# Four modulation vectors of layer 0: from TensorE pieces to row products on VectorE

## The chip, the core and the metric

One Trainium2 chip, one core. The metric is the device time of one execution in microseconds (us), median of several runs. Engines are written PE (TensorE), ACT (ScalarE), DVE (VectorE), POOL (GpSimd) and SP (SyncE); each works through its own list of instructions in a fixed order. In a matmul row, "psg<-wr,cv" reads: into the PSUM tile psg, moving operand wr, stationary operand cv.

## The reference, cut to what matters

A first block (retention and a linear recurrence) gives x. Then two layers of a transformer work on x and on a context xc of 256 tokens each, width 1024. Each layer draws six vectors per sequence out of a condition vector; they scale, shift and gate the activations:

```python
for l in range(DEPTH_2):
    mod = (jax.nn.silu(c) @ w_mod[l] + b_mod[l])[:, None, :]      # 1024 x 6144
    mod_c = jax.nn.silu(c_ctx) @ w_mod[l] + b_mod[l]
    sh1, sc1, ga1, sh2, sc2, ga2 = jnp.split(mod, 6, axis=-1)
    csh1, csc1, cga1, csh2, csc2, cga2 = jnp.split(mod_c, 6, axis=-1)
    h = modulate(rms_norm_2(x, g_pre_mix[l]), sh1, sc1)           # and hc
    ...                                                           # mLSTM, GQA and NA branches, merged into o
    x = x + ga1 * rms_norm_2(o, g_post_mix[l])
    f = conv_ffn(modulate(rms_norm_2(x, g_pre_ffn[l]), sh2, sc2), w_up[l], conv_w[l], conv_b[l], w_down[l])
    x = x + ga2 * rms_norm_2(f, g_post_ffn[l])
```

The change is about ga1, sh2, sc2 and ga2 (numbers m = 2 to 5) of layer 0, for both condition vectors. The first, ga1, is needed only behind the mixers, the last only behind the feed-forward part.

## The kernel before, in words

Everything is fp32. A weight matrix is read in tiles of 128x1024 (512 KB) into `wr` (four buffers) by a DMA on SP's queue; ACT makes a rounded high part `wh` (L106), DVE the rest `wl` (L107), and PE forms three products for each pair of operands (`mm3`, L123 to L125). "The weights' split" below is this L106 and L107. Activations have the same two parts, `hh` and `hl`.

A layer's mixers run one behind the other: `gqa`, `mlstm`, `na`. Beside them runs a list of fillers (`Work`, with a `load` and a generator of short pieces): 24 gate matmuls (`gates`, weights `w_zg`, about 5 us of PE each, called zs in the code), the projections of the branches, and the modulation pieces. `fill(us)` steps fillers until their nominal microseconds are used up; `attend` calls it once for each of its 27 steps with `fills[1]`, and `gqa` once ahead of it with `fills[0]` (the table `FILLS`, L26). Instructions are written in program order, and the scheduler of the framework puts each engine's list in an order by that and by when it reckons the operands to be there; so PE's list around a wait is filled ahead of the run, and a late operand is then a wait.

**A modulation piece** (`modulation`, L363 to L394): for vector m and row block kt, a DMA on SP brings 128x1024 raw weights into `wr`, and four fp32 matmuls (L382) with the two condition vectors as a stationary 128x32 tile `cv` add to a PSUM bank. Behind the eighth piece ACT copies the bank out (L387) and `mod_end` (L409) turns it with two transposes (L419), adds `b_mod` (L423) into `modT`, and forms the gain (m = 1, 4) or the gate row (m = 2, 5; L433 to L438, with a transpose and a small DMA on POOL). Of layer 0, m = 0 and 1 are done in the first block; the 32 pieces of m = 2 to 5 are mixed into the gate matmuls, two to a gate, and run within `gqa`. `y` (the output of each mixer) has its two parts in the tiles yh and yl, six buffers each.

**The stages in time** (of the profile below): up to 240 us the first block; 240 to 281 us the queries and keys of `gqa` of layer 0 (q1, k1, k0, q0 in the code: 1 is the context, 0 is x; L839 to L904 and L808 to L883), in which DVE normalizes, rotates and splits them (`hs`) for PE to transpose (L881 keys, L902 queries); 281 to 431 us its attention with fillers; 431 to about 590 us `mlstm`, of which 431 to 508 are projections and 508 on its four heads; then `na`.

Of the kernel before, what the change touches and what calls it, by code (L numbers as in the profile page):

```python
# [25 lines left out]
FILLS = [(8.0, 3.6, 5.0), (4.0, 1.8, 2.5)]  # L26
# [4 lines left out]
STOCK_Y, STOCK_FIRST = 6, 2  # L31
NPARAM = 0
# [40 lines left out]
class Kern:  # L73
    def __init__(self, tc, A, es):
        self.tc, self.nc, self.A, self.es = tc, tc.nc, A, es
        self.n = 0
        self.cp = es.enter_context(tc.tile_pool(name="const", bufs=1))
        self.hp = es.enter_context(tc.tile_pool(name="h", bufs=1))
# [103 lines left out]
    def gemm_wide(self, src, x, seqs, order=None, at=None, parts=None):  # L182
# [7 lines left out]
        for i, k0 in enumerate(order):  # L190
# [27 lines left out]
    def step(self):  # L218
# [11 lines left out]
        try:  # L230
            self.credit -= next(self.cur[1])
# [131 lines left out]
    def modulation(self, l, pool=None):  # L363
# [3 lines left out]
        def load(m, kt):  # L367
            raw = self.mods[m * KT + kt].tile
# [3 lines left out]
            for i, t in enumerate(raw):  # L372
                self.nc.sync.dma_start(out=t, in_=self.A[f"w_mod{l}"][m * KT + kt][:, i * n : (i + 1) * n])
# [17 lines left out]
        self.mods = [Work(0.45, lambda w, m=m, kt=kt: piece(w, m, kt), lambda m=m, kt=kt: load(m, kt), ahead=l == 0 and m < 2) for m in range(6) for kt in range(KT)]  # L391
        self.fillers += self.mods

    def stock(self, works, pool, n, y=False):  # L394
# [3 lines left out]
        for w in some:  # L398
            if y:
                w.tile = [self.tl(pool, [P, 512], t, 6) for t in ("yh", "yl")]  # L400
            else:
                w.tile = [self.tl(pool, [P, 1024], "stock", n)]
        return some

    def fetch(self, works):
# [4 lines left out]
        return works  # L410

    def mod_end(self, l, m, row):
# [9 lines left out]
        for r in range(2):  # L422
            nc.vector.tensor_tensor(dst[:, :, :, r], src[:, :, :, r], bm[:, m * 8 : (m + 1) * 8].rearrange("p (j b) -> p j b", b=2), ALU.add)  # L423
        i = m // 3
        kind = ("mix", "ffn")[i]
        v = mt[:, 8 * m : 8 * m + 8]
        if m % 3 == 1:
            for r in range(2):
                nc.vector.scalar_tensor_tensor(self.sc[l][:, i, r], v[:, :, r], 1.0, self.param(f"g_pre_{kind}_2{l}"), ALU.add, ALU.mult)
        if m % 3 == 2:  # L430
            gg = self.tl(self.cp, [P, 2, 8], "mgate", 2)
            for r in range(2):
                nc.vector.tensor_tensor(gg[:, r], v[:, :, r], self.param(f"g_post_{kind}_2{l}"), ALU.mult)  # L433
            pt = self.bank("t", 2)
            nc.tensor.transpose(pt[:16, :P], gg.rearrange("p r k -> p (r k)"), self.idn)
            out = self.fs()[:16, :P]
            nc.vector.tensor_copy(out, pt[:16, :P])
            nc.gpsimd.dma_start(out=self.gd[l][2 * i : 2 * i + 2].rearrange("a (k p) -> (a k) p", p=P), in_=out)  # L438
# [5 lines left out]
    def first_block(self):  # L444
        nc, A, tc = self.nc, self.A, self.tc
        with ExitStack() as es:
# [45 lines left out]
            rest = self.fillers[2 * KT :]  # L492
            del self.fillers[2 * KT :]
# [59 lines left out]
            self.fillers += rest  # L553
# [224 lines left out]
    def new_y(self, nq):  # L778
        return [(self.tl(self.ap, [P, nq], "yh", 6, F32R), self.tl(self.ap, [P, nq], "yl", 6, F32R)) for _ in range(4)]

    def gqa(self, l, qs, fills):
        nc, A = self.nc, self.A
        y = self.new_y(len(qs) * T)
        with ExitStack() as es:
# [163 lines left out]
            self.attend(gp, [pair(s, pr) for s in qs for pr in range(4)], fills[1])  # L948
        return y
# [104 lines left out]
    def mlstm(self, l, qs, fills):  # L1054
        nc, A = self.nc, self.A
        y = self.new_y(len(qs) * T)
        nq = len(qs) * T
        with ExitStack() as es:
            mp = es.enter_context(self.tc.tile_pool(name=f"ml{l}", bufs=1))
            mlmask = self.load(mp, [P, 2, P], "mlmask", A["ml_mask"])  # L1060
# [49 lines left out]
            def prepare(h):  # L1110
# [17 lines left out]
                nc.scalar.activation(k, ps, AF.Copy, scale=P**-0.5)  # L1128
                return ub, dg, q, k
# [33 lines left out]
            self.require(self.br[0])  # L1163
            for s in qs:
                ss = self.tl(mp, [P, 8], "mss", 2)
                for t in range(2):
                    for h in range(4):
                        junk = self.tl(mp, [P, P], "mjunk", 1)
# [6 lines left out]
                for hp in range(2):  # L1175
# [380 lines left out]
```

## Time and profile before

| | |
|---|---|
| median of 3 runs | 1768.2 us (1767.57 to 1769.2) |
| the profiled execution, its own time | 1768.12 us |
| its span, first to last instruction | 1766.3 us |
| PE busy | 1730.1 us, 98% |
| DVE / ACT / POOL busy | 1118.3 (63%) / 877.4 (50%) / 130.0 us (7%) |
| granted TensorE clock, mean | 0.996 |
| share of PE in the chain that ended last | 86% |

A busy PE here counts each matmul from its start to its modelled end; matmuls overlap, so what one costs is read from the distance between starts. Busy shares are averages over stages; the sections below go by stage.

### The profile page before, as it was taken

The numbers are of one execution on the slowest core, as the hardware profiler recorded it, in microseconds if no ns is written. First come the engines' busy times: TensorE is split into PE (matmuls) and PEld (weight loads), VectorE is DVE, ScalarE is ACT, GpSimd is POOL, SyncE is SP. The second block draws the span as 40 slices with busy tenths as digits, with TensorE's granted clock in tenths as the row PEclk, the third lists the DMA queues.
The fourth block names the chain that finished last, engine by engine and source line by source line (L and its number), as shares of the span: only waits on it lengthen the run. The fifth ranks groups of instructions, "written<-read, shape, count | busy, mean of one in ns | idle before, by whom it ended". The sixth has DMA issues, their size and how long they took to land.

```text
span 1766.3 us, 27570 instructions
## 1 busy us (share of the span) xinstructions
PE 1730.1 (98%) x10512; PEld 1465.8 (83%) x10512; DVE 1118.3 (63%) x2159; ACT 877.4 (50%) x1597; POOL 130.0 (7%) x126
## 2 busy tenths in 40 slices
PE   7999999999999999999999999999999999989998
PEld 6889887777888887787778888888889888879987
DVE  7978676444435687558556663369744578578864
ACT  6665554344435455335434442346654456456652
POOL 2210000000100010000101110000010000002210
PEclk9999999999999999999999999999999999999999
DMA  8864544666334332553454334454446545876573
GB/s 300 292 202 146 168 157 154 213 197 224 120 115 137 114 106 87 171 198 138 166 171 130 100 102 137 132 188 146 136 140 201 160 149 159 294 243 191 180 226 106
DMA packets 111381, 295.66 MB, mean 167 GB/s; under 512 B 28144, under 2 KB 37936, under 8 KB 110992
## 3 DMA queue, kind: packets, MB, share of 16 engines
q1 hardware_dynamic: 110544, 292.96, 51.3%
q8 instruction: 83, 1.36, 0.3%
q0 software_dynamic: 272, 0.36, 0.1%
q10 hardware_dynamic: 432, 0.57, 0.1%
q14 instruction: 50, 0.41, 0.1%
HBM read 278.05 MB, written 19.46 MB: 168 GB/s over the span
## 4 chain that ended last, share of the span: by engine, by line
PE 86%; DVE 7%; DMA 3%; ACT 2%; issue 1%; SPq 1%; POOL 0%; DVEq 0%; ACTq 0%; POOLq 0%
PE psg L123 25%; PE psg L125 24%; PE psg L124 24%; DVE wl L107 2%; PE psg L764 2%; PE psg L382 2%; PE pst L750 2%; PE pst L1155 1%; PE pss L938 1%; PE pss L1027 1%; PE pss L1143 1%; DMA fs<-sigd 1%; DMA wr<-in_w_in_dram 1%; ACT wh L106 1%; DMA wr<-in_w_up_dram 1%
## 5 line engine op out<-in xcount | busy, mean ns | idle before, releaser
L107 DVE TENSOR_TENSOR wl<-wr,wh 128x1024 fp32r<-128x1024 f32 x359 | 443.9, 1239 | 319.4 <-ACT wh L106 306.4
L106 ACT CAST wh<-wr 128x1024 fp32r<-128x1024 f32 x360 | 375.8, 1045 | 414.2 <-PE psg L124 164.0
L123 PE MATMUL psg<-hh,wh 128*128 128x256 f32 (+1 forms) x1712 | 570.6, 334 | 1.6 <-ACT hh L322 1.0
L125 PE MATMUL psg<-hh,wl 128*128 128x256 f32 (+1 forms) x1712 | 562.7, 329 | 2.0 <-DVE wl L107 1.6
L124 PE MATMUL psg<-hl,wh 128*128 128x256 f32 (+1 forms) x1712 | 564.5, 330 | 0.0
L123 PEld LDWEIGHTS psg<-hh,wh 128*128 128x128 f32 x1712 | 325.7, 191 | 48.0 <-issue 11.4
L125 PEld LDWEIGHTS psg<-hh,wl 128*128 128x128 f32 x1712 | 325.5, 190 | 33.3 <-DVE wl L107 2.5
L124 PEld LDWEIGHTS psg<-hl,wh 128*128 128x128 f32 x1712 | 325.9, 190 | 28.3 <-DVE rstd L277 0.8
L123 PE MATMUL psg<-wh,hh 128*128 128x512 f32 (+1 forms) x320 | 118.7, 371 | 1.5 <-ACT fs L331 1.5
L124 PE MATMUL psg<-wl,hh 128*128 128x512 f32 (+1 forms) x320 | 118.5, 370 | 0.0
L125 PE MATMUL psg<-wh,hl 128*128 128x512 f32 (+1 forms) x320 | 118.4, 370 | 0.0
L1401 POOL TENSOR_TENSOR u<-u 128x512 f32<-128x512 f32 (+1 forms) x44 | 61.4, 1395 | 671.1 <-DVE u L1356 671.1
L125 PE MATMUL psg<-wh,midl 128*128 128x512 f32 (+1 forms) x276 | 101.6, 368 | 0.0
L123 PE MATMUL psg<-wh,midh 128*128 128x512 f32 (+1 forms) x276 | 101.5, 368 | 0.0
L124 PE MATMUL psg<-wl,midh 128*128 128x512 f32 (+1 forms) x276 | 101.5, 368 | 0.0
L1352 ACT ACTIVATE u<-psg,prm 128x256 f32<-128x256 f32 (+1 forms) x92 | 59.7, 649 | 27.9 <-PE psg L125 27.9
L123 PEld LDWEIGHTS psg<-wh,hh 128*128 128x128 f32 x320 | 60.4, 189 | 11.5 <-ACT fs L331 1.7
L731 ACT ACTIVATE p<-pss,sm 128x512 f32<-128x512 f32 x64 | 43.9, 687 | 49.9 <-DVE sm L730 49.7
L125 PEld LDWEIGHTS psg<-wh,hl 128*128 128x128 f32 x320 | 60.5, 189 | 9.7
L124 PEld LDWEIGHTS psg<-wl,hh 128*128 128x128 f32 x320 | 60.3, 189 | 9.6
L123 PE MATMUL psg<-yh,wh 128*128 128x512 f32 (+1 forms) x192 | 65.4, 341 | 0.0
L125 PE MATMUL psg<-yh,wl 128*128 128x512 f32 (+1 forms) x192 | 64.9, 338 | 0.0
(315 smaller groups left out, 2507.4 us busy)
## 6 DMA issues: line engine op xcount, KB each, us to landing
wr<-in_w_up_dram SPq DMA_DIRECT2D x88, 512.0 KB, 3.7
wr<-in_w_mod_dram SPq DMA_DIRECT2D x55, 512.0 KB, 4.1
wr<-in_w_zg_dram SPq DMA_DIRECT2D x48, 512.0 KB, 4.1
wr<-in_w_in_dram SPq DMA_DIRECT2D x40, 512.0 KB, 4.7
wr<-in_w_dw_dram SPq DMA_DIRECT2D x40, 512.0 KB, 3.5
wr<-in_w_br_dram SPq DMA_DIRECT2D x24, 512.0 KB, 3.5
stock<-in_w_mod_dram SPq DMA_DIRECT2D x19, 512.0 KB, 6.5
v<-in_w_mod_dram SPq DMA_DIRECT2D x16, 512.0 KB, 4.3
```

Source lines behind the costliest of these rows:

```text
L106: nc.scalar.copy(hi, raw)
L107: self.last_lo = (eng or nc.vector).tensor_tensor(lo, raw, hi.bitcast(F32), ALU.subtract).ins
L123: mm(ps, a[0], b[0], start=first, stop=False)
L124: mm(ps, a[0], b[1], start=False, stop=False)
L125: mm(ps, a[1], b[0], start=False, stop=last)
L382: nc.tensor.matmul(ps[32 * j : 32 * j + 32, 0:T], self.cv[:, kt], raw[j], start=kt == 0, stop=kt == KT - 1)
L731: nc.scalar.activation(t, s, AF.Exp, bias=m, accum_out=z)
L750: nc.tensor.transpose(pt[:, k * P : (k + 1) * P], t[:, k * P : (k + 1) * P], self.idn)
L764: nc.tensor.matmul(po[64 * j : 64 * j + 64, :T], p[2](j, k), pTs[id(p), j][:, k], start=k == 0, stop=k == nk - 1)
L938: nc.tensor.matmul(ps, qT[s, pr][:, j, qt * P : (qt + 1) * P], kT[kv][:, c, s * T : 512], start=c == 0, stop=c == 1)
L1352: nc.scalar.activation(u, ps, AF.Identity, scale=cw[:, 1, n : n + 1], bias=cb[:, n : n + 1])
L1401: nc.gpsimd.tensor_tensor(a, a, b, ALU.mult)
```

## The change

The pieces of m = 2 to 5 of layer 0 leave TensorE. Their weights are laid out transposed on the host (`w_mt0`: a row of 1024 inputs for each of the outputs, 128 outputs to a tile, 32 tiles of 512 KB). For each tile and each of the two condition vectors DVE runs one `scalar_tensor_tensor` (tile x 0.5 x row, with its sum over 1024 elements into a column of `modT`): 64 products. The row is silu(c) twice over, broadcast to 128 partitions, made by `mod_rows` within `gqa`: two DMAs on SP, four tanh on ACT, four DVE operations. The tiles come in through two buffers (`mw`) by DMAs on POOL's queue; a load waits for the two products that read the tile before it in its buffer. `tick` counts the nominal microseconds of fillers and of some matmuls of `mlstm`, and writes a product for each `PACE` = 3.0 of them, with an edge behind the last weights' split written until then. `y` becomes one tile of 1024 with six buffers, of which the two `mw` are the fifth and sixth. `FILLS[0][1]` falls from 3.6 to 3.1, and the gates stand in the list without modulation pieces. Layer 1 keeps its TensorE pieces.

```diff
-FILLS = [(8.0, 3.6, 5.0), (4.0, 1.8, 2.5)]
+FILLS = [(8.0, 3.1, 5.0), (4.0, 1.8, 2.5)]
+MK, MT = ((0, 1), range(6)), ((2, 3, 4, 5), ())
+PACE = 3.0
...
+            self.tick(2.7 * len(seqs))                       # gemm_wide, per weight tile
...
+            us = next(self.cur[1])                           # step
+            self.credit -= us
+            self.tick(us)
...
-        self.mods = [... for m in range(6) for kt in range(KT)]
+        self.mods = [... for m in MK[l] for kt in range(KT)]
...
+    def mod_rows(self, todo):
+        nc, A = self.nc, self.A
+        self.cb = []
+        for r in range(2):
+            c = self.row(self.up, "u", A["c_rows"][r : r + 1], D, 2)
+            for h in range(2):
+                d = slice(h * 512, (h + 1) * 512)
+                t = self.fs()
+                self.tanh2(t, c[:, d])
+                nc.vector.scalar_tensor_tensor(c[:, d], t, 1.0, c[:, d], ALU.add, ALU.mult)
+            self.cb.append(c)
+        self.todo = [(l, m, j, rs) for l, m, rs in todo for j in range(8)]
+        self.held = []
+        self.mw = [self.tl(self.ap, [P, 1024], "y", 6) for _ in range(2)]
+
+    def hold(self):
+        if self.todo:
+            l, m, j, rs = self.todo.pop(0)
+            w = self.mw[len(self.todo) % 2]
+            self.nc.gpsimd.dma_start(out=w, in_=self.A[f"w_mt{l}"][MT[l].index(m) * 8 + j])
+            self.held.append((w, l, m, j, list(rs)))
+
+    def tick(self, us):
+        if self.junk is None or not self.todo and not self.held:
+            return
+        self.since += us
+        while self.since > PACE and (self.todo or self.held):
+            self.since -= PACE
+            self.product()
+
+    def product(self):
+        while self.todo and len(self.held) < 2:
+            self.hold()
+        w, l, m, j, rs = self.held[0]
+        r = rs.pop(0)
+        with self.tc.issue_after(self.last_lo):
+            self.nc.vector.scalar_tensor_tensor(self.junk, w, 0.5, self.cb[r], ALU.mult, ALU.mult, accum_out=self.modT[l][:, m * 8 + j, r : r + 1])
+        if not rs:
+            self.held.pop(0)
+            self.hold()
+            if j == 7:
+                both = (0, 1)
+                for r in both:
+                    v = self.modT[l][:, 8 * m : 8 * m + 8, r]
+                    self.nc.vector.tensor_tensor(v, v, self.param(f"b_mod_2{l}")[:, m * 8 : m * 8 + 8], ALU.add)
+                self.mod_use(l, m, both)
...
-                order = (q1, k1, behind(q1), k0, behind(k1), q0, k1, k0, q1, q0, k0, fill(fills[0]), q0)
+                order = (q1, k1, behind(q1), k0, behind(k1), q0, k1, k0, q1, rows(), q0, k0, junk(), fill(fills[0]), q0)
```

**On PE**, where the first gates of `gqa` meet: the gate's PSUM tile is the first psg of a group, L123 to L125 (L128 to L130 after) are its three products. Before:

```order
L123 MATMUL psg_3263<-hh_112,wh_3259 128x512
L124 MATMUL psg_3263<-hl_113,wh_3259 128x512
L125 MATMUL psg_3263<-hh_112,wl_3260 128x512
L382 MATMUL psg_3293<-wr_3291,cv 32x256 x4
L382 MATMUL psg_3293<-wr_3298,cv 32x256 x4
L123 MATMUL psg_3310<-hh_112,wh_3302 128x512
L124 MATMUL psg_3310<-hl_113,wh_3302 128x512
L125 MATMUL psg_3310<-hh_112,wl_3303 128x512
```

After, where a gate's matmuls follow a score and the next gate comes behind it:

```order
L128 MATMUL psg_3396<-hh_112,wh_3317 128x512
L129 MATMUL psg_3396<-hl_113,wh_3317 128x512
L130 MATMUL psg_3396<-hh_112,wl_3318 128x512
L1012 MATMUL pss_3434<-akT_2752,aqT_3347 128x512 x2
L128 MATMUL psg_3453<-hh_112,wh_3392 128x512
L129 MATMUL psg_3453<-hl_113,wh_3392 128x512
L130 MATMUL psg_3453<-hh_112,wl_3393 128x512
```

The pieces are gone and nothing stands in their place; of all PE's instructions 128 of L382 and 8 transposes of L419 are missing, no other is added or gone, and from the last head of `mlstm` on the order is the same but for these names.

**On DVE**, in the queries' and keys' stretch at 252 to 268 us: hss are sums of squares, rstd the steps of a root, wl a split, hs the parts that PE transposes. Before, from the square sums of k1 on:

```order
L815 TENSOR_TENSOR p_3049<-psg_2884,hss_3030 128x128 x2
L107 TENSOR_TENSOR wl_3260<-wr_3257,wh_3259 128x1024
L818 TENSOR_TENSOR p_3049<-p_3049,gqk 128x256
L808 TENSOR_REDUCE hss_3134<-p_3135 128x4
L258 TENSOR_SCALAR rstd_558_3138<-hss_3134 128x4
L873 TENSOR_TENSOR hs_3053<-p_3049,hs_3053 128x4x64 x2
```

After, the rows of the condition vectors ahead of it, and then the same place:

```order
L904 TENSOR_REDUCE hss_2941<-p_2945 128x8
L431 SCALAR_TENSOR_TENSOR u_3193<-fs_3195,u_3193 128x512
L266 TENSOR_SCALAR rstd_525_2948<-hss_2941 128x16
L431 SCALAR_TENSOR_TENSOR u_3193<-fs_3198,u_3193 128x512
...
L431 SCALAR_TENSOR_TENSOR u_3201<-fs_3206,u_3201 128x512
...
L883 TENSOR_TENSOR p_3045<-p_3045,gqk 128x256
L266 TENSOR_SCALAR rstd_554_3134<-hss_3130 128x4
L112 TENSOR_TENSOR wl_3281<-wr_3278,wh_3280 128x1024
L938 TENSOR_TENSOR hs_3049<-p_3045,hs_3049 128x4x64 x2
```

Four products of 512 columns stand ahead of the context queries' root, and more splits (wl) stand ahead of the hs: four to k1's, six to k0's, where three and four stood.

**On DVE**, where the attention of `gqa` begins (sm is a softmax maximum, sz its sum, p the probabilities; y here is a tile of w_mt0). Before:

```order
L894 TENSOR_TENSOR hs_3242<-p_3234,hs_3242 128x8x64
L107 TENSOR_TENSOR wl_3387<-wr_3384,wh_3386 128x1024
L730 TENSOR_REDUCE sm_3352<-pss_3351 128x1
L732 RECIPROCAL sz_3353<-sz_3353 128x1
L733 TENSOR_SCALAR p_3354<-p_3354,sz_3353 128x512
```

After:

```order
L959 TENSOR_TENSOR hs_3256<-p_3248,hs_3256 128x8x64
L464 SCALAR_TENSOR_TENSOR hs_3271,modT_87<-y_3210,u_3193 128x1024
L464 SCALAR_TENSOR_TENSOR hs_3271,modT_87<-y_3210,u_3201 128x1024
L464 SCALAR_TENSOR_TENSOR hs_3271,modT_87<-y_3209,u_3193 128x1024
L795 TENSOR_REDUCE sm_3371<-pss_3370 128x1
L795 TENSOR_REDUCE sm_3404<-pss_3403 128x1
L464 SCALAR_TENSOR_TENSOR hs_3271,modT_87<-y_3209,u_3201 128x1024
L797 RECIPROCAL sz_3372<-sz_3372 128x1
L797 RECIPROCAL sz_3405<-sz_3405 128x1
L464 SCALAR_TENSOR_TENSOR hs_3271,modT_87<-y_3210,u_3193 128x1024
L798 TENSOR_SCALAR p_3373<-p_3373,sz_3372 128x512
```

Products stand between a maximum and its reciprocal, where DVE waits for ACT's exponential. Of the 64, 30 lie in `gqa`, 23 in the projections of `mlstm` and 11 in its first heads.

## Rows read from the trace of the kernel before

**Rows 1.** The page's busy times; then PE's waits from 281 to 590 us.

```profile
PE 1730.1 (98%) x10512; PEld 1465.8 (83%) x10512; DVE 1118.3 (63%) x2159; ACT 877.4 (50%) x1597; POOL 130.0 (7%) x126
...
PE pst L902 <- ACT aqT L904: 0.3, 1, 0.3
```

**Rows 2.** Busy us by stage: PE, PEld, DVE, ACT, POOL, clock, DMA, GB/s.

```profile
265.00:281.00 16.00, 15.68 (x84) 12.46 (x82) 15.07 (x53) 8.29 (x16) 0.00 (x0) 1.00 0.28 88
281.00:431.00 150.00, 149.67 (x940) 107.58 (x940) 68.24 (x129) 64.19 (x132) 1.08 (x2) 1.00 0.63 209
431.00:508.00 77.00, 77.00 (x347) 63.22 (x344) 28.75 (x33) 31.55 (x49) 7.92 (x8) 1.00 0.40 123
500.00:590.00 90.00, 89.84 (x526) 77.38 (x524) 50.93 (x142) 46.02 (x151) 5.17 (x4) 1.00 0.36 120
```

**Rows 3.** L382 alone (PE, PEld); PE in time order: start, us, line, operands.

```profile
280.00:431.00 151.00, 17.96 (x256) 6.27 (x256) 1.00 0.62 207
...
280.64 0.39 PE L124 MATMUL psg<-hl,wh 128*128 128x512 f32 x1
280.87 0.39 PE L125 MATMUL psg<-hh,wl 128*128 128x512 f32 x1
281.19 1.07 PE L382 MATMUL psg<-wr,cv 128*32 128x256 f32 x16
...
282.53 0.40 PE L124 MATMUL psg<-hl,wh 128*128 128x512 f32 x1
...
308.96 0.40 PE L419 MATMUL pst<-idn,fs 128*128 128x128 f32 x2
309.12 0.48 PE L124 MATMUL psg<-hl,wh 128*128 128x512 f32 x1
...
314.96 0.64 PE L382 MATMUL psg<-wr,cv 128*32 128x256 f32 x8
315.53 0.66 PE L750 MATMUL pst<-idn,p 128*128 128x128 f32 x4
```

**Rows 4.** Groups by form: line, operation, count, busy us, mean ns, idle before.

```profile
L1214 DVE SCALAR_TENSOR_TENSOR res<-o,prs,res 128x1024 f32<-128x1024 f32 x6 | 7.4, 1281 | 0.0
L1402 DVE SCALAR_TENSOR_TENSOR fs<-fs,u 128x512 f32<-128x512 f32 x22 | 15.2, 692 | 30.5 <-POOL u L1401 30.5
L279 DVE SCALAR_TENSOR_TENSOR rstd<-rstd,rstd 128x1 f32<-128x1 f32 x52 | 7.3, 155 | 0.1
L107 DVE TENSOR_TENSOR wl<-wr,wh 128x1024 fp32r<-128x1024 f32 x42 | 51.4, 1224 | 84.2 <-ACT wh L106 84.1
```

**Rows 5.** ACT, DVE and PE in time order around the keys of layer 0.

```profile
254.54 0.37 ACT L867 COPY av<-psg 128x256 f32<-128x256 f32 x1 [2.38 <-PE psg L125]
...
266.79 0.76 DVE L873 TENSOR_TENSOR hs<-p,hs 128x256 fp32r<-128x256 f32 x2
...
273.87 0.76 DVE L873 TENSOR_TENSOR hs<-p,hs 128x256 fp32r<-128x256 f32 x2
...
271.01 1.03 PE L881 MATMUL pst<-idn,hs 128*128 128x128 f32 x8
...
275.77 1.14 PE L881 MATMUL pst<-idn,hs 128*128 128x128 f32 x8
```

**Rows 6.** The softmax chain in the attention, groups by form as in rows 4.

```profile
L730 DVE TENSOR_REDUCE sm<-pss 128x1 f32<-128x512 f32 x16 | 11.0, 687 | 11.3 <-PE pss L938 11.2
L732 DVE RECIPROCAL sz<-sz 128x1 f32<-128x1 f32 x16 | 2.6, 162 | 9.4 <-ACT p L731 9.4
```

**Rows 7.** Loads: SP's from the page; then POOL's L438 and gqk, with landing.

```profile
wr<-in_w_mod_dram SPq DMA_DIRECT2D x55, 512.0 KB, 4.1
...
L438 POOL DMA_DIRECT2D gd<-fs x4: 526/544/559, 310.9 to 1577.5; - x4
...
DMA to landing us min/median/max: 1.6/3.5/5.0
...
DMA to landing us min/median/max: 7.6/7.6/7.6
```

More of the change, by code (lines that the diff above doesn't have):

```diff
@@ L367, in load @@
         def load(m, kt):
-            raw = self.mods[m * KT + kt].tile
+            raw = self.mods[MK[l].index(m) * KT + kt].tile
             if raw is None:
@@ L389, in piece @@
             self.mod_end(l, m, row)
-        self.mods = [Work(0.45, lambda w, m=m, kt=kt: piece(w, m, kt), lambda m=m, kt=kt: load(m, kt), ahead=l == 0 and m < 2) for m in range(6) for kt in range(KT)]
+        self.mods = [Work(0.45, lambda w, m=m, kt=kt: piece(w, m, kt), lambda m=m, kt=kt: load(m, kt), ahead=l == 0 and m < 2) for m in MK[l] for kt in range(KT)]
         self.fillers += self.mods
@@ L399, in stock @@
             if y:
-                w.tile = [self.tl(pool, [P, 512], t, 6) for t in ("yh", "yl")]
+                w.tile = [self.tl(pool, [P, 1024], "y", 6)]
             else:
@@ L423, in mod_end, with mod_use @@
             nc.vector.tensor_tensor(dst[:, :, :, r], src[:, :, :, r], bm[:, m * 8 : (m + 1) * 8].rearrange("p (j b) -> p j b", b=2), ALU.add)
+        self.mod_use(l, m, (0, 1))
+    def mod_use(self, l, m, rs):
+        nc = self.nc
         i = m // 3
         kind = ("mix", "ffn")[i]
-        v = mt[:, 8 * m : 8 * m + 8]
+        v = self.modT[l][:, 8 * m : 8 * m + 8]
         if m % 3 == 1:
-            for r in range(2):
+            for r in rs:
                 nc.vector.scalar_tensor_tensor(self.sc[l][:, i, r], v[:, :, r], 1.0, self.param(f"g_pre_{kind}_2{l}"), ALU.add, ALU.mult)
@@ L431, in mod_end @@
             gg = self.tl(self.cp, [P, 2, 8], "mgate", 2)
-            for r in range(2):
+            n = len(rs)
+            for r in rs:
                 nc.vector.tensor_tensor(gg[:, r], v[:, :, r], self.param(f"g_post_{kind}_2{l}"), ALU.mult)
             pt = self.bank("t", 2)
[L435 to L438, printed above, removed]
+            nc.tensor.transpose(pt[: 8 * n, :P], gg[:, :n].rearrange("p r k -> p (r k)"), self.idn)
+            out = self.fs()[: 8 * n, :P]
+            nc.vector.tensor_copy(out, pt[: 8 * n, :P])
+            nc.gpsimd.dma_start(out=self.gd[l][2 * i : 2 * i + n].rearrange("a (k p) -> (a k) p", p=P), in_=out)
     def shift(self, l, i, s):
@@ L778, in new_y @@
     def new_y(self, nq):
-        return [(self.tl(self.ap, [P, nq], "yh", 6, F32R), self.tl(self.ap, [P, nq], "yl", 6, F32R)) for _ in range(4)]
+        return [(y[:, 0], y[:, 1]) for y in (self.tl(self.ap, [P, 2, nq], "y", 6, F32R) for _ in range(4))]
     def gqa(self, l, qs, fills):
@@ L923, in gqa, with rows, junk @@
                 q1, k1, k0, q0 = queries(1, pq, at={3: lambda: next(put(self.yx, 0))}), keys((1,), pk), keys((0,), pk), queries(0, None, (pq, 2))
-                order = (q1, k1, behind(q1), k0, behind(k1), q0, k1, k0, q1, q0, k0, fill(fills[0]), q0)
+                def rows():
+                    self.mod_rows([(0, m, (0, 1)) for m in MT[0]])
+                    yield
+                def junk():
+                    self.junk = self.tl(gp, [P, 8, 2, 64], "hs", 3, F32R).bitcast(F32).rearrange("p a b c -> p (a b c)")
+                    yield
+                order = (q1, k1, behind(q1), k0, behind(k1), q0, k1, k0, q1, rows(), q0, k0, junk(), fill(fills[0]), q0)
             else:
@@ L1059, in mlstm @@
             mp = es.enter_context(self.tc.tile_pool(name=f"ml{l}", bufs=1))
+            self.products(mp, l)
             mlmask = self.load(mp, [P, 2, P], "mlmask", A["ml_mask"])
@@ L1315, in layer @@
             if l == 0:
+                assert not self.todo and not self.held
                 self.modulation(1)
```

29 lines of the change are left out of this document (17 added, 12 removed).

## The prediction, made before the changed kernel ran

> **What bounds the kernel now.** I read the busy times and PE's waits first, then the stages, then PE in time order around the pieces that go. PE is busy 98% of the span, and from 281 to 590 us it waits 0.3 us in all, once, for ACT [rows 1]. The table of stages says the same of each stage that the change touches: PE 149.67 of 150.00 us in the attention of `gqa`, 77.00 of 77.00 in the projections of `mlstm`, 89.84 of 90.00 on its heads, at a granted clock of 1.00 [rows 2]. DVE is busy 68.24 of 150, 28.75 of 77 and 50.93 of 90 us there. So in these stages the length is PE's work, and DVE has some 82 and 48 us free in the first two. The reader should see the exception too: from 265 to 281 us DVE is busy 15.07 of 16.00 us [rows 2]. There PE is covered by little.
>
> **What goes from PE.** Between 280 and 431 us L382 has 256 records, PE busy 17.96 us [rows 3]; two records are one fp32 matmul, so that is 128 matmuls, the 32 pieces. That busy time leaves out what the change of shape costs, so I take starts. An ordinary matmul of the gate starts 0.23 us behind the one before (280.64 to 280.87). From the L125 at 280.87 to the L124 at 282.53 there are 1.66 us, and two ordinary steps lie in it (L125's own and that of an L123 between): 1.66 - 0.46 = 1.20 us for two pieces together (x16) [rows 3]. A piece alone (x8) holds PE from 314.96 to 315.53, 0.57 us, with a change of shape on both sides that is partly there anyway [rows 3]. In the timeline 12 pairs and 8 single pieces stand: 12 x 1.20 + 8 x 0.57 = 14.4 + 4.6 = 19.0. The two transposes of L419 take 0.16 us to the next start (308.96 to 309.12) [rows 3], four times 0.6. Together 19.6; with a tenth of a microsecond for each single piece's edges 20.4. I take 20, ends 18 (the busy time alone) and 21. PE is dense there, so all of it lies on the path, and the listed order shows that no other PE instruction is added or lost. The lower `FILLS` moves no work: 27 steps x 0.5 = 13.5 nominal us less, against 32 x 0.45 = 14.4 nominal us of pieces that are gone, so the gates fall where they fell.
>
> **What comes onto DVE.** 64 products of 128x1024 with two fp32 inputs from SBUF. The trace has the same operation and shape without the sum, 1281 ns; a plain two-input operation of that shape takes 1224 [rows 4]. No DVE operation of the trace writes a sum beside its result. If reading it out is a small operation of its own, it adds about the 155 ns of one on 128x1 [rows 4]: 1.44. From below, 1.22; from above I allow twice the nearest row, 2.56. I take 1.28, since that row differs in nothing but the sum: 64 x 1.28 = 82 us.
> By stage: 30 in the attention of `gqa` are 38.4, and 68.2 + 38.4 = 106.6 us of a stage that shrinks to 150 - 20 = 130: 82% busy. 23 in the projections of `mlstm`: 28.75 + 29.4 = 58.2 of 77: 76%. 11 on the first heads: 14 us, where some 40% is free. It all fits beside PE by sums. DVE works in order, so the question is what waits behind a product: the next maximum and multiply of a softmax, and the next weights' split. The edge behind the last split keeps a product from standing ahead of it, and the splits run ahead by up to four buffers. The softmax has two steps of `attend` between the score and its transposes; a step is 130/27 = 4.8 us. Its chain on DVE is 0.69 for the maximum, 0.16 for the reciprocal [rows 6] and a multiply, with ACT's exponential between (the 9.4 us of idle ahead of 16 reciprocals, 0.6 each, are the wait for it [rows 6], and the order puts products there). Two products and a split inside it are 3.8 us more, about 6 us of some 9. So most hide. For what doesn't I take 1 us, ends 0 and 6.
>
> **What the front pays.** The condition rows need four tanh on ACT and four DVE operations of 128x512 at 0.69 us [rows 4], and the order puts these ahead of the root of the context queries, where DVE is full. ACT's part falls into 2.38 us in which it waits at 254.54 for PE [rows 5]; DVE waits perhaps 1 us for the two rows to land and the first tanh. Besides, without pieces in `wr` the gates' weights come sooner, and the order puts one split more (1.22 us [rows 4]) ahead of k1's hs, two ahead of k0's. So k1's hs, ready at 266.79 + 0.76 = 267.55, come 4 x 0.69 + 1 + 1.22 = 5.0 us later, at 272.5; PE reaches their transposes at 271.01 [rows 5]: a wait of 1.5. k0's come 5.0 + 1.22 = 6.2 us later than 273.87 + 0.76 = 274.63, at 280.8. PE reaches them at 275.77 [rows 5] + the 1.5 + 1.6 for seven more gate matmuls that the order puts ahead = 278.9: 1.9 more. Behind that, the order has 23 more gate matmuls ahead of the first score than before, 5 us, which cover the rest. I take 3 us, ends 0 (the rows land early, PE's slack holds) and 6 (every lag seen by PE).
>
> **The queues.** SP gives up 32 loads of 512 KB and gets two of a row broadcast; its loads weren't waited for by PE, so I count nothing. POOL gets 32 issues at 0.54 us (L438 [rows 7]), 17 us on an engine busy 9 us from 281 to 508 [rows 2]. Its `dg` tiles of `mlstm` stand in the same queue behind loads that wait for products; they are needed on the heads, some 40 us after the operands come, which covers a few products. A load must be there when DVE reaches it, or DVE and all behind it stands. With a product each 130/30 = 4.3 us in `gqa` and 77/23 = 3.35 us in `mlstm`, and two products to a tile, the time from the last reader of a buffer to the first of its next tile is three intervals less a product: 11.6 and 8.8 us. The trace has no load of this size from POOL. SP's of the same bytes land in 4.1 us; POOL's small ones in 1.6 to 5.0, and one in the crowded start in 7.6 [rows 7]. With the issue 2.1 to 8.2 us: below 8.8, so nothing, and I keep 4.6 (SP's) as likeliest. Bunches at the start of the attention (five products around two maxima) may wait for the third tile; that is in the 1 us above.
>
> **The sum.** 1768.1 (the profiled execution, span 1766.3 and 1.8 around it; the median is 1768.2, so no correction) - 20 + 3 + 1 = 1752. Bounds: 1768.1 - 21 = 1747 with nothing lost; 1768.1 - 18 + 6 + 6 = 1762.
>
> **Rivals.**
> *The products cost twice as much, and the kernel is slower.* At 2.56 us DVE would need 68.2 + 30 x 2.56 = 145 of 130 us in `gqa`, 28.75 + 23 x 2.56 = 87.6 of 77 in `mlstm`'s projections, and on the heads (about 47 us, 26.6 busy) 26.6 + 11 x 2.56 = 54.8: 15 + 10.6 + 7.8 = 33 us too much, in which PE waits for splits and softmax: 1768.1 - 20 + 3 + 33 = 1784. The point from which it is slower is a product of about 2.3 us (64 x 2.3 - 129 = 18 eats what is left of the gain). Against it: 1281 ns for the same inputs [rows 4]; for it: the sum is what that row lacks. [...] Chance 0.06.
> *DVE is too dense for a queue in order.* At 82% each step of the attention may be late a little: 0.4 us on 24 units are 10 us, 1762. For it: 265 to 281 us, where DVE is 94% busy and PE holds only 0.3 us; against it: PE has no wait at all in `mlstm`'s heads with DVE at 57%, and the order fills ACT's gaps. Chance 0.15.
> *POOL's loads land late.* From 8.2 us after the issue on DVE waits in `mlstm`; at 12 us each tile is 3.7 us late, 11 tiles 43 us, of which 19 are DVE's free time there: 24 lost, 1775. Against it: every landing in rows 7 is shorter. [...] Chance 0.04.
>
> **Chances and range.** Forecast 1752, chance 0.75, its own range 1747 to 1762. The rivals hold 0.06, 0.15 and 0.04. Two tenths of a per cent are 3.5 us, about what a measurement tells from no change: 1764.7 to 1771.7 is the same. Faster: 0.75 and most of the dense case, 0.11: 0.86. Same: the rest of it and some of the late loads: 0.06. Slower: 0.08. For 8 in 10 the range goes from 1746 to 1763, which takes in the forecast's own and a part of the dense case.
>
> **What the profile will show.** L382 has no rows between 281 and 431 us; `gqa`'s attention is about 130 us long, with PE still dense. The products' group has 64 rows of 1.2 to 1.5 us; 2.5 means the first rival. PE waits around 270 to 282 us for DVE's hs, some 3 us together. Idle time of DVE ahead of products put down to the DMA of y means the third rival; PE waiting for wl or for p inside the attention means the second. From 600 us on the stages are as long as before, shifted. Wrong would be the forecast if PE's waits from 245 to 560 us came to over 10 us.

## The result, and the profile after

The changed kernel takes 1745.32 us (1744.67 to 1745.76, 4 runs), the kernel before beside it 1767.88 us (1766.51 to 1769.2, 4 runs): a ratio of 0.9869, 95% interval 0.9858 to 0.9881. The forecast was 1752.0 with a range from 1746 to 1763. So the direction and the mechanism were right, and the gain is 22.6 us instead of 16; the time lies 0.7 us below the range. The profiled execution has 1744.95 us, a span of 1743.1 and a mean granted clock of 0.997.

The page of the changed kernel, busy times and the load of the new tiles, which answer to rows 1 and 7 (KB each, us from issue to landing; then the spread of the landing):

```profile
PE 1707.9 (98%) x10248; PEld 1458.0 (84%) x10248; DVE 1188.4 (68%) x2291; ACT 878.1 (50%) x1597; POOL 149.0 (9%) x158
...
y<-in_w_mt_dram POOLq DMA_DIRECT2D x32, 512.0 KB, 4.5
...
DMA to landing us min/median/max: 3.7/4.5/9.0
```

PE's waits from 240 to 600 us (us in total, times, longest), and the busy us by stage (PE, PEld, DVE, ACT, POOL, clock, DMA share, GB/s): the attention of `gqa` (first with the 12 us ahead of its first score, as in [rows 2], then without), the projections of `mlstm`, its heads.

```profile
PE pst L946 <- ACT hs L936: 0.6, 1, 0.6
PE pst L315 <- issue: 0.3, 1, 0.3
PE pst L967 <- DVE hs L959: 0.3, 1, 0.3
PE pst L1256 <- DVE hb L1251: 0.2, 1, 0.2
...
281.00:411.00 130.00, 129.74 (x678) 102.46 (x678) 99.53 (x187) 61.15 (x128) 8.46 (x16) 1.00 0.52 166
293.00:411.00 118.00, 118.00 (x620) 93.16 (x620) 87.73 (x163) 55.26 (x119) 8.46 (x16) 1.00 0.53 171
411.00:489.00 78.00, 78.00 (x352) 63.96 (x351) 57.30 (x85) 31.07 (x49) 13.39 (x19) 1.00 0.64 198
489.00:570.00 81.00, 80.74 (x486) 69.50 (x486) 58.78 (x167) 44.48 (x147) 9.01 (x9) 1.00 0.46 147
```

PE is as dense as before [rows 2], in an attention that is shorter: it ended at 431 us and ends at 411. DVE went from 45% to 77% busy there (99.53 of 130 us, where the prediction had 82%) and from 37% to 73% in the projections, and PE's waits are 1.4 us in 360.

The products (count: ns min/median/max, first and last start), what DVE waited for ahead of them, and who waited for them:

```profile
L464 DVE SCALAR_TENSOR_TENSOR junk<-y,u x34: 1207/1219/1493, 413.3 to 529.3; 128x1024 f32<-128x1024 f32 x34
L464 DVE DVE_READ_ACCUMULATOR junk<-y,u x34: 72/83/86, 414.4 to 530.4; 128x1 f32 x34
...
  DMA y<-in_w_mt_dram: 11.5, 5
...
  POOL y L442: 113.6, 13
```

A product is 1.22 us and a small read of 0.08 behind it. DVE did stand 11.5 us in front of tiles that had not landed, five times; PE shows nothing of it.

The front on DVE, in time order (start, us, and in brackets the idle time ahead), with "..." where rows are left out:

```profile
253.81 0.69 DVE L431 SCALAR_TENSOR_TENSOR u<-fs,u 128x512 f32<-128x512 f32 x1 [0.56 <-ACT fs L339]
254.42 0.17 DVE L266 TENSOR_SCALAR rstd<-hss 128x16 f32<-128x16 f32 x1
254.50 0.68 DVE L431 SCALAR_TENSOR_TENSOR u<-fs,u 128x512 f32<-128x512 f32 x1
255.10 0.17 DVE L274 TENSOR_SCALAR rstd<-rstd 128x16 int32<-128x16 int32 x1
255.18 0.68 DVE L431 SCALAR_TENSOR_TENSOR u<-fs,u 128x512 f32<-128x512 f32 x1
...
256.46 0.17 DVE L279 TENSOR_TENSOR rstd<-rstd 128x16 f32<-128x16 f32 x1
256.66 0.17 DVE L280 TENSOR_TENSOR rstd<-rstd,rstd 128x16 f32<-128x16 f32 x1
...
258.34 1.29 DVE L908 TENSOR_TENSOR p<-psg,hss 128x512 f32<-128x512 f32 x2
...
269.96 0.76 DVE L938 TENSOR_TENSOR hs<-p,hs 128x256 fp32r<-128x256 f32 x2
...
277.37 0.76 DVE L938 TENSOR_TENSOR hs<-p,hs 128x256 fp32r<-128x256 f32 x2
```

The reader should look at the distances: a step of the root starts 0.20 us behind the one before (256.46, 256.66) and is 0.17 long, so the chain of dependent steps is paid by their starts. Where a row operation stands between two steps, the two together take 0.68 (254.42 to 255.10). Four row operations and their wait moved the multiply behind the root by 2.4 us: it starts at 258.34, and in the kernel before at 255.90.

```profile
255.90 1.29 DVE L843 TENSOR_TENSOR p<-psg,hss 128x512 f32<-128x512 f32 x2
```

### The profile page after: what moved, and what is told of

It is laid out like the page before. It is cut to its first block, busy times and chain, and to the rows that moved or that the text cites. A ratio compares the mean times of both kernels' runs of the same rounds, so it can differ in the third digit from the quotient of the medians.

```text
span 1743.1 us, 27235 instructions
## 1 busy us (share of the span) xinstructions
PE 1707.9 (98%) x10248; PEld 1458.0 (84%) x10248; DVE 1188.4 (68%) x2291; ACT 878.1 (50%) x1597; POOL 149.0 (9%) x158
## 4 chain that ended last, share of the span: by engine, by line
PE 86%; DVE 7%; DMA 3%; ACT 2%; issue 1%; POOL 0%; DVEq 0%; ACTq 0%; POOLq 0%; SPq 0%
PE psg L128 25%; PE psg L129 25%; PE psg L130 25%; PE psg L829 2%; DVE wl L112 2%; PE pst L815 2%; PE pst L1231 1%; PE pss L1012 1%; PE psg L390 1%; PE pss L1102 1%; PE pss L1219 1%; PE pst L315 1%; DMA wr<-in_w_up_dram 1%; PE pst L811 0%; DMA wr<-in_w_o_dram 0%
## 5 line engine op out<-in xcount | busy, mean ns | idle before, releaser
L128 PE MATMUL psg<-hh,wh 128*128 128x256 f32 (+1 forms) x1712 | 567.9, 333 | 1.7 <-ACT hh L330 1.2
L130 PE MATMUL psg<-hh,wl 128*128 128x256 f32 (+1 forms) x1712 | 561.9, 329 | 1.1 <-DVE wl L112 1.1
L128 PEld LDWEIGHTS psg<-hh,wh 128*128 128x128 f32 x1712 | 325.1, 190 | 42.0 <-issue 7.7
L130 PEld LDWEIGHTS psg<-hh,wl 128*128 128x128 f32 x1712 | 325.3, 190 | 31.4 <-DVE wl L112 1.4
L128 PE MATMUL psg<-wh,hh 128*128 128x512 f32 (+1 forms) x320 | 119.0, 372 | 1.4 <-ACT fs L339 1.4
L130 PE MATMUL psg<-wh,hl 128*128 128x512 f32 (+1 forms) x320 | 118.4, 370 | 0.0
L130 PE MATMUL psg<-wh,midl 128*128 128x512 f32 (+1 forms) x276 | 101.6, 368 | 0.0
L128 PE MATMUL psg<-wh,midh 128*128 128x512 f32 (+1 forms) x276 | 101.5, 368 | 0.0
L128 PEld LDWEIGHTS psg<-wh,hh 128*128 128x128 f32 x320 | 60.4, 189 | 11.4 <-ACT fs L339 1.7
L130 PEld LDWEIGHTS psg<-wh,hl 128*128 128x128 f32 x320 | 60.4, 189 | 9.7
L1432 DVE SCALAR_TENSOR_TENSOR u<-psg,prm,u 128x255 f32<-128x255 f32 (+1 forms) x92 | 54.6, 594 | 20.0 <-ACT u L1429 19.9
L128 PE MATMUL psg<-y,wh 128*128 128x512 f32 (+1 forms) x192 | 65.4, 340 | 0.2 <-DVE fs L1359 0.2
```

Of the source, the lines that this page charges most:

```text
L128: mm(ps, a[0], b[0], start=first, stop=False)
L130: mm(ps, a[1], b[0], start=False, stop=last)
L1432: nc.vector.scalar_tensor_tensor(u3[:, :, 1:], p3[:, :, : T - 1], cw[:, 0, n : n + 1], u3[:, :, 1:], ALU.mult, ALU.add)
```

## The experiments

The kernel before ran beside each group of runs: 1767.74 us (1765.04 to 1770.48) beside the first four, 1767.01 (1765.36 to 1770.02) beside the next four, 1767.19 (1765.77 to 1768.8) beside the next three, 1767.52 (1766.77 to 1769.01) beside the last.

**Nothing in place of the pieces.** The changed kernel without condition rows, loads and products.

```diff
+        nc.gpsimd.memset(self.modT[0][:, 16:48], 0.0)
-        for r in range(2):                                   # mod_rows
+        for r in range(0):
-            self.nc.gpsimd.dma_start(out=w, in_=self.A[f"w_mt{l}"][...])
-        with self.tc.issue_after(self.last_lo):
-            self.nc.vector.scalar_tensor_tensor(self.junk, w, 0.5, self.cb[r], ...)
```

> The changed kernel with the 64 products, their 32 loads and the four rows' operations left out (m = 2 to 5 of layer 0 are then only the bias): what is left of the change is PE without its pieces. Theory A (the products are hidden, and the front's wait that the prediction feared is not there): the time is that of the changed kernel, 1745.3, down to 1744 for the 0.6 us of PE's waits at 277 and 286 us. Rival B (the prediction's own: losses of 3 us at the front and 1 in the attention are in the 1745.3, and more went from PE than 20): 1741 or less.

Measured: 1745.42 us (1745.26 to 1746.77), ratio 0.9875 (0.986 to 0.989). The changed kernel has 1745.32 with all of it: what the change adds costs nothing that can be measured. The first theory holds.

**Each product twice.**

```diff
-            self.nc.vector.scalar_tensor_tensor(self.junk, ...)
+            for _ in range(2):
+                self.nc.vector.scalar_tensor_tensor(self.junk, ...)
```

> Each product is issued twice (same result): what the prediction's rival of a product at twice the price would have done. By the sums DVE then needs 93 + 30 x 1.3 = 132 us in the 118 us of gqa's attention and 57 + 23 x 1.3 = 87 in the 78 of mlstm's projections: if DVE in order is then the bound, about 24 us more, 1769, with PE waiting for wl and p. If the prepared order and the four weight buffers soak it up, under 1755.

Measured: 1759.19 (1758.31 to 1760.47), ratio 0.9953 (0.9941 to 0.9966). Its stages, columns as above, and its longest wait of PE:

```profile
293.00:411.00 118.00, 118.00 (x609) 91.98 (x608) 114.41 (x218) 54.31 (x119) 7.96 (x15) 1.00 0.48 151
411.00:489.00 78.00, 76.83 (x344) 62.01 (x343) 75.89 (x112) 31.35 (x50) 17.71 (x17) 1.00 0.58 197
489.00:570.00 81.00, 73.47 (x436) 63.75 (x434) 76.89 (x163) 37.99 (x115) 12.12 (x12) 0.98 0.51 163
...
PE pst L1232 <- DVE md L1229: 7.5, 3, 4.9
```

The time lies between the two that were expected. DVE is 95 to 97% busy in all three stages, and even so the attention's PE is full; PE loses its time on the heads. In the changed kernel DVE has 30.3 + 20.7 + 22.2 = 73 us free there, and 64 more products of 1.30 are 83: 10 too many by the sum, 14 measured. So what was paid is about what DVE's time is short of; a dense queue as such cost the attention nothing, with DVE 97% busy there. And at 2.6 us a product the kernel is still faster than before; the prediction had put the point of no gain at 2.3.

**No edge behind the split.**

```diff
-        with self.tc.issue_after(self.last_lo):
-            self.nc.vector.scalar_tensor_tensor(self.junk, ...)
+        self.nc.vector.scalar_tensor_tensor(self.junk, ...)
```

> The products without the edge behind the last weights' split; the order then puts up to four products in a row ahead of two splits in the projections of mlstm. Theory A (DVE has room and splits run ahead by buffers): same, 1745 to 1747. Rival (the edge is what hides the products): PE waits for wl in mlstm, 1750 or more.

Measured: 1757.77 (1755.84 to 1761.08), ratio 0.9946 (0.9933 to 0.9959), 12.5 us over the changed kernel. PE's waits and the projections' stage:

```profile
PE psg L129 <- DVE wl L112: 4.1, 1, 4.1
PE psg L130 <- DVE wl L112: 4.0, 2, 2.3
...
411.00:489.00 78.00, 71.65 (x315) 57.89 (x312) 65.53 (x96) 29.30 (x47) 17.36 (x23) 0.98 0.62 199
```

DVE ahead of the wait of 4.1 us, and POOL beside it:

```profile
444.71 2.20 DVE L463 SCALAR_TENSOR_TENSOR junk<-y,u 128x1024 f32<-128x1024 f32 x1 [4.04 <-DMA y<-in_w_mt_dram]
...
451.47 2.16 DVE L463 SCALAR_TENSOR_TENSOR junk<-y,u 128x1024 f32<-128x1024 f32 x1
...
454.01 1.22 DVE L112 TENSOR_TENSOR wl<-wr,wh 128x1024 fp32r<-128x1024 f32 x1
...
444.52 5.82 POOL L1192 TENSOR_TENSOR dg<-ub,mlmask 128x512 f32<-128x512 f32 x3 [4.16 <-DMA ub<-ud]
```

The theory that the edge makes little difference falls. Without it products run ahead of splits up to the next tile that hasn't landed, and a split that PE needs stands behind a product that waits: here behind 4.04 us for a tile and four products. These four took 2.16 to 2.22 us each instead of 1.22, beside POOL's `dg`: another 4 us. With the edge DVE stands about as long for tiles (11.5 us in five places, against 14.2 in eleven), and PE sees nothing of it. It isn't that DVE is busier: at PACE 2.5 (below) it is 64.70 us busy in this stage, against 65.53 here, and 2.5 us are lost.

**The loads on SP's queue.**

```diff
-            self.nc.gpsimd.dma_start(out=w, in_=self.A[f"w_mt{l}"][...])
+            self.nc.sync.dma_start(out=w, in_=self.A[f"w_mt{l}"][...])
```

> The 32 loads on SP's queue and not POOL's. In SP's queue a load that waits for a product holds back the weights behind it. Theory A (weights are there long before their use): within 2 us of 1745. Rival (the own queue is what lets the loads wait without harm): weights come late, PE waits for wl, 1755 or more.

Measured: 1746.88 (1746.23 to 1748.0), ratio 0.9884 (0.987 to 0.9897): 1.6 us over the changed kernel, in the first theory's range; the intervals of the two ratios overlap. The queue of its own is worth little.

**The first term alone.** The kernel before without its 32 pieces, the vectors constant.

```diff
-            rest = self.fillers[2 * KT :]
+            rest = []
```

> The kernel before, with the 32 pieces of vectors 2 to 5 of layer 0 left out and nothing put in their place: their loads on SP, 128 matmuls, 8 transposes and the copies and gates behind them are gone, and the vectors are constants. FILLS stays at 3.6, the yh and yl tiles and all else are as before. It measures the first term of the sum, the one called 20 us, alone. Theory A, the term was sized right and what the changed kernel gained beyond it comes from the order of the gates in the heads of mlstm (FILLS, fewer changes of shape), some 1 us, and from a stretch at a lower granted clock in one profile: 1747 to 1748, 20 to 21 under the kernel before. Rival B, the pieces cost more than their matmuls' starts show (buffers of wr, SP's loads, shapes): 1745 or less, 22 to 23 under. Rival C, the changed kernel has its extra gain from another part of the change (y as one tile, new_y later): over 1749.

Measured: 1747.51 (1746.35 to 1748.36), ratio 0.9889 (0.9875 to 0.9902): 19.5 us under the kernel before. The time is the first theory's, but with FILLS at 3.6 the gates have moved as well; the last experiment separates the two.

**The rows alone.** The changed kernel with the rows, without loads and products (the edit of the first experiment without its `range(0)`).

> The changed kernel with the two condition rows (two DMAs, four tanh, four operations of 128x512 on DVE) where they stand, but with no loads of w_mt0 and no products; the four vectors are constants. Beside the kernel without rows, loads and products (1745.42) it measures the front alone. Theory A, the root's short steps wait for each other's results and leave DVE gaps, so that the rows' operations lie in them and reach PE with under 1 us: 1745 to 1746.4. Rival B, the term of the prediction, 3 us that something else then gives back: 1748.4.

Measured: 1746.47 (1746.19 to 1746.7), ratio 0.9883 (0.987 to 0.9897). 1.0 us over the kernel without rows, less than these intervals resolve, and not 3; the first theory was just missed at its upper end. In its trace PE waits 1.2 us for the `hs` of k0, where the changed kernel waits 0.6. That the changed kernel, with products on top, is some 1.1 us faster than this one is not explained.

**FILLS back at 3.6.**

```diff
-FILLS = [(8.0, 3.1, 5.0), (4.0, 1.8, 2.5)]
+FILLS = [(8.0, 3.6, 5.0), (4.0, 1.8, 2.5)]
```

> The changed kernel with FILLS[0][1] at 3.6 again, so that one part of the change is undone: each of the 27 steps of the attention asks for 0.5 nominal us more, and gates move from the mlstm and na stages into gqa. Theory A, only the place of gates moves, and the heads of mlstm, which have fewer gates to mix in, lose the 0.8 us that the trace shows them to have gained, and a little more: 1746 to 1748. Rival B, the order of the gates has nothing to do with the gain: within 0.5 of 1745.3. Rival C, the stage that runs out of gates is left with waits that nothing covers: 1750 or more, with PE waiting for ACT or DVE on the heads or in na.

Measured: 1757.11 (1754.01 to 1758.62), ratio 0.9945 (0.9931 to 0.9958): 11.8 us are gone, the time of the third theory. PE's one long wait, DVE ahead of it, and the loads that were on their way:

```profile
PE pst L1231 <- DVE md L1228: 5.7, 1, 5.7
...
523.01 0.08 DVE L464 DVE_READ_ACCUMULATOR junk<-y,u 128x1 f32 x1
529.20 1.23 DVE L464 SCALAR_TENSOR_TENSOR junk<-y,u 128x1024 f32<-128x1024 f32 x1 [6.11 <-DMA y<-in_w_mt_dram]
...
531.49 1.22 DVE L464 SCALAR_TENSOR_TENSOR junk<-y,u 128x1024 f32<-128x1024 f32 x1
...
532.63 2.21 DVE L1228 TENSOR_TENSOR md<-pss,md 128x384 f32<-128x384 f32 x4
...
518.33 0.62 SPq L1034 DMA_DIRECT2D rpbd<-in_rpb_dram  x1
519.36 0.55 POOL L442 DMA_DIRECT2D y<-in_w_mt_dram  x1 [5.86 <-DVE junk L464]
...
rpbd<-in_rpb_dram SPq DMA_DIRECT2D x1, 1792.0 KB, 10.0
```

Three products within 5 us use up both tiles, DVE stands 6.11 us for the next one, and `md` of a head of `mlstm` stands behind it. The bunch alone doesn't make these 6 us: the load was issued 3.7 us before DVE was free for its tile, so that the median landing of 4.5 us would have cost some 0.8. It took 9.7, beside a load of 1792 KB that SP had issued 1.0 us earlier; that this load is the reason was not tested. The mean granted clock from 489 to 570 us is 0.96 there, against 1.00: at most 81 x 0.04 = 3.2 us, which with the wait of 5.7 come to 8.9 of the 9.1 by which the profiled execution is longer.

**FILLS at 3.6 and PACE at 2.6.**

```diff
-PACE = 3.0
+PACE = 2.6
```

> FILLS[0][1] at 3.6 as in the run before, which came to 1757, but with PACE 2.6 instead of 3.0: the same 64 products, the last of them ahead of the second head of mlstm instead of on it. Theory A, those 12 us were one place, a product on the heads that waits 6 us for its tile with the head's md behind it on DVE, so that PE stands 5.7 us and its clock falls: without products there 1746 to 1748. Rival B, gates that move out of the heads leave them uncovered by themselves: 1754 or more, with PE waiting for md again.

Measured: 1748.63 (1748.14 to 1749.82), ratio 0.9893 (0.9877 to 0.991). 8.5 of the 11.8 us are back, and PE's wait for that `md` is gone: most of it was the product on the heads, not the place of the gates. A new wait of 2.1 us for `md` of the gate vectors (L1147) at the start of the projections came with it, and 0.6 are over the first theory's range.

**PACE at 2.5, FILLS at 3.1.**

> The changed kernel with PACE 2.5 instead of 3.0 and nothing else: 64 products, denser in gqa and in the projections of mlstm, none behind the first head. Theory A, the pace itself is not what limits while DVE has room (some 80% busy in gqa): within 1 of 1745.3. Rival B, at 2.5 the second tile's load lands behind its user more often and a split waits behind it: 1748 or more, with PE waiting for wl in the projections.

Measured: 1747.77 (1746.1 to 1749.22), ratio 0.9889 (0.9874 to 0.9904). Between the two theories; the added wait is 1.5 us for the same L1147. PACE at 3.0 is about as dense as the products go for nothing.

**Six vectors, and five.** Two vectors, then one, of layer 1 as products too.

```diff
-MK, MT = ((0, 1), range(6)), ((2, 3, 4, 5), ())
-PACE = 3.0
+MK, MT = ((0, 1), range(2, 6)), ((2, 3, 4, 5), (0, 1))       # five: range(1, 6), (0,)
+PACE = 2.0                                                   # five: 2.4
```

> Two vectors more: m = 0 and 1 of layer 1 leave TensorE too (16 pieces) and become 32 products behind the 64 of layer 0, with PACE at 2.0 so that 96 fit into the same stretch. By the price of a pair of pieces (1.2 us) PE loses 9.6 us more. Each product twice cost 14 us for 64 extra ones. Theory A, the loss grows steeply only where DVE is full, so 32 extra ones cost 3 to 5: 1739 to 1741, faster than both kernels. Rival B, the cost is in proportion, 7 us, and some of layer 1's pieces covered waits behind the mixers anyway, so they were worth less than 9.6: 1743 to 1746. Rival C, at PACE 2.0 a load's landing no longer fits between two users of its buffer, DVE waits for the DMA of y in mlstm: over 1748.

> One vector more (m = 0 of layer 1: 8 pieces less on TensorE, 16 products more, 80 in all) at PACE 2.4. By the price of a pair of pieces PE loses 4.8 us. The kernel with six vectors lost the 9.6 it should have gained and 3.3 more: 13 us for 32 extra products. Theory A, that loss came from single places where a tile of w_mt lands late at the denser pace and DVE stands in front of a split, and at 2.4 there are few: 1741 to 1743. Rival B, each product beyond 64 costs 0.4 us whatever the pace: 1745.3 - 4.8 + 6.4 = 1747.

Measured: six 1748.61 (1747.53 to 1751.22), ratio 0.9898 (0.9884 to 0.9911); five 1745.24 (1744.51 to 1746.68), ratio 0.9876 (0.9861 to 0.9891). Five are as fast as four: no gain. PE's longest wait of six from 240 to 800 us, and then, of five and of the changed kernel, PE at the first matmul of the heads and at the first piece of layer 1 that is read out of `wr`:

```profile
PE psg L129 <- DVE wl L112: 3.9, 1, 3.9
```

```profile
493.13 1.05 PE L1219 MATMUL pss<-mq,mk 128*128 128x128 f32 x8
...
834.36 0.85 PE L390 MATMUL psg<-wr,cv 128*32 128x256 f32 x12
```

```profile
489.06 1.16 PE L1219 MATMUL pss<-mq,mk 128*128 128x128 f32 x9
...
829.14 1.07 PE L390 MATMUL psg<-wr,cv 128*32 128x256 f32 x16
```

With five the heads begin 4.1 us later and this piece comes 5.2 us later, while the span is only 0.4 us longer (1743.5 against 1743.1): behind that point five take 4.8 us less. So the price of a piece holds (4.8 us for eight, as expected), and 16 products more cost some 4 us up to the heads. The other 1.1 up to the pieces need not be theirs: the granted clock is 0.91 from 800 to 820 us in this execution, and 1.00 in the changed kernel's. It isn't DVE's busy time, 96.89 us of 118 in the attention: DVE waits 19.1 us in front of tiles in nine places, against 11.5 in five of the changed kernel, and PE 2.3 us for splits in the projections. Neither theory for five has its number; the rival's, a price whatever the pace, is as near as the first. Six came out as its third theory says, and the clock adds to it: it is 0.95 from 440 to 460 us, behind PE's long wait, and 0.91 from 520 to 540, and 1.00 in the changed kernel in both places.

**The first term with the gates in their place.** As the experiment on the first term, with `FILLS[0][1]` at 3.1.

> The kernel before without the 32 pieces (the four vectors are constants), as in the run that came to 1747.5, and with FILLS[0][1] at 3.1 as in the changed kernel instead of 3.6. So the gates keep the places in time that they have in the kernel before; at 3.6 two to three gates more run in gqa and the heads of mlstm began at 503.6 us, at 3.1 in the changed kernel at 489.1. The changed kernel without rows and products came to 1745.4. Theory A, these 2 us are the place of the gates, which the prediction counted at nothing: 1745 to 1746. Rival B, they come from the rest of the change (y as one tile, new_y later, gates listed without pieces): 1747 to 1748 again.

Measured: 1745.26 (1744.37 to 1746.25), ratio 0.9873 (0.9856 to 0.9889): 22.3 us under the kernel before, and 0.1 under the changed kernel. The first theory holds: the 2 us between this run and the one at 3.6 are the place of the gates. What they consist of is open, since PE's waits from 240 to 800 us come to 1.9 us here and to 2.0 there.

## Why the prediction was wrong in size, step by step

**What bounds the kernel** was read rightly: PE, before and after.

**The step that failed is the size of the sum's terms: the 3 for the front above all, then the 20 for the pieces and the 1 for the products.** Measured were 0 to 1.0, 22.3 and 0. Against 1752 the kernel is 6.7 us faster: 3 for the front and 1 for the products that were not paid, 2.3 that PE gave back beyond 20, and 0.4 of rounding and of medians.

*"I take 3 us" for the front* was the largest miss: the rows alone cost 1.0 us at most, and the whole change costs 0.1 us beyond the run without pieces. Three numbers of that step were too high. A lag of 4 x 0.69 + 1 = 3.8 us from the row operations was 2.4, since they start 0.68 us apart with a step of the root between, for which the chain would have paid 0.2 anyway, and the wait for the first tanh was 0.56. A split more ahead of k1's hs was taken at its full 1.22, beside a root that leaves DVE free between its steps: it added 0.7. So k1's hs came at 269.96 + 0.76 = 270.72 instead of 272.5, and PE took its transposes up right there, with no wait. k0's came at 277.37 + 0.76 = 278.13 instead of 280.8, and PE waited 0.6 us instead of 1.9 (L946, above; for the half of hs that ACT makes from the same p). The prediction had written the end at 0 for "PE's slack holds", and took the middle between two ends instead of following the chain step by step, which the rows of before allowed.

*"For what doesn't I take 1 us"* for products that don't hide was 0 to within the intervals.

*"I take 20" for the pieces* was right for the stage that it was worked out from. PE at the first matmul of the heads and at the first piece of layer 1 out of `wr`, in the kernel before and then in the one without pieces and with FILLS at 3.1:

```profile
508.74 1.50 PE L1143 MATMUL pss<-mq,mk 128*128 128x128 f32 x12
...
851.17 1.07 PE L382 MATMUL psg<-wr,cv 128*32 128x256 f32 x16
```

```profile
488.98 1.28 PE L1146 MATMUL pss<-mq,mk 128*128 128x128 f32 x10
...
829.21 1.07 PE L382 MATMUL psg<-wr,cv 128*32 128x256 f32 x16
```

19.8 us are gone up to the heads, 22.0 up to layer 1's pieces, and 23.0 at the end of the span (1766.3 to 1743.3). So some 3 us came behind the stage, where the prediction said "as long as before, shifted". Part is the clock: in the profile of the kernel before it was granted at 0.89 from 815 to 830 us, in the run without rows and products from 800 to 815, in the changed kernel and in the one without pieces at 1.00 in that place. The rows are of the kernel before, of the run without rows and products, and of the changed kernel:

```profile
815.00:830.00 15.00, 12.97 (x94) 12.11 (x93) 13.17 (x40) 7.31 (x16) 0.00 (x0) 0.89 0.18 72
```

```profile
800.00:815.00 15.00, 13.09 (x96) 12.40 (x95) 11.32 (x32) 8.88 (x17) 0.00 (x0) 0.89 0.06 10
```

```profile
800.00:815.00 15.00, 12.93 (x103) 12.07 (x102) 12.33 (x39) 8.51 (x17) 0.00 (x0) 1.00 0.04 13
```

15 x 0.11 = 1.65 us at most, at the same work with PE idle some 2 us in it. Since a kernel without the pieces shows it too, it goes with the execution and not with the change. It belongs to the 23.0 of this pair of traces rather than to the medians: among the runs of the last experiment whose mean clock is 0.997, three on either side, the gain is still 22.2 us (1767.20 and 1744.96 on average). So the 2.3 beyond 20 aren't explained by the clock. In the traces what is left is about 0.6 on the heads and `na` and 1.0 at the end; it was read from one pair and stays open.

*"The lower FILLS moves no work"*: true at 3.1, and what was not seen is what it guards. Left at 3.6 it would have cost 2 us without products (1747.51 against 1745.26) and 11.8 with them.

**The rivals.** *A product twice as dear* did not happen: one of the 64 took 1.49 us, beside POOL's `dg`, the others about 1.22. With its two fp32 sources and its sum a product took 1.22 us, against 1.28 without the sum [rows 4], and the read of the sum is 0.08 of its own. Its price was overrated as well: 33 us by the prediction's stages, 14 measured with doubled products, since products that find no room run on into the heads and beyond. *DVE too dense for a queue in order*: not at 77%; the edge is what keeps it so, and without it 12.5 us are lost. *POOL's loads land late*: the median landing was 4.5 us as forecast (4.6), and at PACE 3.0 the five waits of DVE for tiles are hidden. The mechanism is real, though, and both grounds on which it was ruled out fail. The spacing is not even: three products close together use up both tiles at once. And not every landing is shorter than 8.2 us: the longest was 9.0 in the changed kernel and 9.7 at FILLS 3.6, where the two met. It decided the run at 3.6 and, by the places of DVE's waits, six vectors.

## What to carry to other kernels

Small work went to an engine that was 40% busy at no cost beside a full TensorE, and may elsewhere, as long as its instructions stand behind those that TensorE needs next; that place in the order was worth 12 us here, the queue that loads it 1 or 2. Two buffers bear an even pace and not a bunch, least of all with landings of twice the median (9.0 and 9.7 us here, against 4.5), so look in the order for the places where several users of a buffer stand in a row, and at what stands behind them. When a chain of small dependent steps is interleaved with wide ones, add what the chain doesn't already pay (here some 0.5 us of a wide one's 0.68), and where the budget of a planner's step loses a part of its work, lower it by as much, or other work moves.

## What the runs showed of the hardware

- A sum written beside a 128x1024 product on DVE appears as an instruction of its own, 0.08 us long, behind a product of 1.22 us.
- Dependent steps of 128x16 elements on DVE start 0.20 us apart at 0.17 us each; with an independent operation of 128x512 between them, itself 0.68 us long, a step and that operation take 0.68 us together: the wide one adds some 0.5.
- The same product beside a POOL operation that reads 128x512 from SBUF took 2.16 to 2.22 us, four in a row, without the edge, while POOL's `dg` ran (5.82 us for three, against 1.31 for one by itself in the changed kernel). Of the changed kernel's 64 products the one of 1.49 us, at 444.38, lies beside a `dg` of 1.74; the other 63 took at most 1.23. With the loads on SP's queue the longest took 2.34.
- A load of 512 KB issued by POOL landed in 4.5 us (median; 3.7 to 9.0), SP's of the same size into `wr` in 3.4 to 4.6 in that kernel (medians by weight); its issue took POOL 0.53 us. On SP's queue the same tiles landed in 3.4 to 10.4, 4.6 in the median, so the long landings aren't POOL's alone. No issue of these tiles took longer than 0.61 us, with DVE 77% busy in the attention; what makes the long landings long was not tested.
- The granted clock was 0.89 over 15 us with gaps of PE of some 2 us in it in one execution, and 1.00 with the same gaps in another. In the first, the kernel before, it was 0.53 from 826.0 to 829.6 us, right behind the gaps, and 1.00 from 829.6 to 832.0: a matmul of 256 columns starts 0.21 us behind the one before in the first stretch (828.60 to 828.81), and 0.12 behind it in the second (829.98 to 830.10).
